# The two parts of the dense products' operand move into one tile at another place of the on-chip memory

## The chip, the cores and the metric

The kernel runs on one core of one Trainium2 chip. The metric is device time in microseconds (us) for one execution: 1100.3 us is the median of three executions before the change.

## What is computed

The reference is two transformer blocks on one sequence of 256 tokens with 1024 features, in float32. Cut to what matters here, every layer is a chain of dense products with attention, scans and convolutions between them:

```python
h = rmsnorm(x, gain)
y = h @ w_in                       # queries, keys, values, gates: thousands of columns
x = x + mix(y) @ w_out             # mix: attention, gated linear attention, convolution
h = rmsnorm(x, gain)
x = x + square(relu(h @ w_up)) @ w_down      # 1024 -> 4096 -> 1024
```

There are three such layers with three MLPs, and a norm at the end.

## The kernel before

Features lie on the 128 partitions, tokens along them: an operand of 1024 features is eight K tiles of 128 features by 256 tokens. The weights come from the chip's main memory as one stream of 128 by 128 blocks, in the order of use, through three 1 MB staging buffers (`stg`, issued from SyncE's queue).

A product in float32 is made of three products in the matrix unit's float32r format. Each weight block is split into a high part `whi` (ScalarE, L168) and a low part `wlo` (VectorE, L170); the operand is split likewise into `xh` and `xl`, by `operand(j, gain)` for K tile j (ScalarE L299, VectorE L300). `gemm` then issues per K tile, back to back: `whi` with `xh` (L225), `whi` with `xl` (L228), `wlo` with `xh` (L229). In each the weight block is loaded (128 columns, a row of its own in the trace, engine PEld), and the operand's K tile of 256 columns streams past it (engine PE).

- `gemm1` and `gemm2` make one or two output tiles by eight K tiles in this way. They serve all projections (`xh`, `xl`), the mixing products (`yc_h`, `ya_h`, `yh_h`, `mh`, `oh`, `cq_h`, `ck_h` and their low parts) and the MLP's first product.
- `gemm_tokens` (L264) turns the roles round: a 128 token piece of `xh` or `xl` is loaded as the weights, and 256 columns of `whi` or `wlo` stream past it.
- `gemm_wide` (L237, L238) serves the MLP's second product, except for the last of its eight output tiles: the hidden values lie in one tile `hid`, with high and low part next to each other for each K tile, so that one matmul takes 512 columns of both.
- The last output tile of the MLP's second product goes through `gemm1` with `hid[:, :, 0]` and `hid[:, :, 1]`.

Side work (attention, scans) is cut in steps that are put in between the tiles of the dense products; its small matmuls run on TensorE between those of the products.

Where things lie. Buffers are laid out one behind the other along each partition in the order in which the program asks for them, each on a multiple of 32 bytes. In the program of before, `xv` (constants and the residual stream, 8504 bytes per partition) comes first at byte 16512, `xh` (8192 bytes) follows at 25024, `xl` at 33216, `cst` at 41408. The five `whi` buffers begin at 76800 and the five `wlo` buffers at 97280, 4096 bytes each; a block of 128 columns is 512 bytes, so every weight block begins on a multiple of 512. The other operands begin at: `oh` 128000, `ol` 136192; `hid` 128000 in the first two MLPs and 136192 in the third; `ya_h`, `ya_l`, `yh_h`, `yh_l`, `yc_h`, `yc_l` from 128000 to 148480 in steps of 4096; `cq_h` 188928, `cq_l` 192000; `ck_h` 201216, `ck_l` 203264; `mh` 204576, `ml` 212768. K tiles of these are 1024 bytes apart (`hid`: 2048).

Of the kernel before, what the change touches and what calls it, by code (L numbers as in the profile page):

```python
# [35 lines left out]
# output tiles of the MLP's second product, from the last, that take one part of the operand at a time  # L36
WN = 1
# columns of the first weights to come
FIRST = 256
# steps of side work per tile of eight blocks, in three places  # L40
# [24 lines left out]
def _mid(ap, n):  # L65
    """[p, f] -> [p, n, f], the same f for each of n."""
    return ap.unsqueeze(1).to_broadcast([ap.shape[0], n, ap.shape[1]])


def _last(ap, n):  # L70
    """[..., f] -> [..., f, n], each of f repeated n times."""
    return ap.unsqueeze(len(ap.shape)).to_broadcast(list(ap.shape) + [n])
# [3 lines left out]
def kernel(  # L76
# [36 lines left out]
    xh = keep.tile([128, KD, T], FP32R, name="xh")  # L113
    xl = keep.tile([128, KD, T], FP32R, name="xl")
# [9 lines left out]
    # the first products want the first K tiles of both operands  # L124
# [29 lines left out]
    def first(chain, ready=4, n=2):  # L154
        """Keep the splits of the weights that come after the next `ready` units behind a chain of small steps."""
        hold[:] = [None] * ready + [chain] * n

    def take(u, pieces=2):
        """The parts of unit u."""
        c, i = divmod(u, CHUNK_UNITS)  # L160
        if c not in staged:
            load(c)
        src = staged[c][:, i * UW:(i + 1) * UW]
        h = whi_p.tile([128, UW], FP32R, name="whi")
        l = wlo_p.tile([128, UW], FP32R, name="wlo")
        n = UW // pieces
        pieces = [slice(q * n, (q + 1) * n) for q in range(pieces)]
        act = [nc.scalar.activation(out=h[:, z], in_=src[:, z], func=AF.Copy)  # L168
               for z in (pieces if u == 0 else [slice(0, UW)])]
        dve = [nc.vector.tensor_tensor(out=l[:, z], in0=src[:, z], in1=h[:, z], op=ALU.subtract) for z in pieces]  # L170
        chain = hold.pop(0) if hold else None
        if chain:
            after(act[0], chain[0])
            after(dve[0], chain[1])
        units.clear()
        units[u] = h, l

    def block(n=1):
        """The parts of the next n blocks, which lie in one unit."""
        b = stream["block"]  # L180
        stream["block"] = b + n
        u, i = divmod(b, UNIT)
        assert i + n <= UNIT
        if u not in units:
            take(u)
        h, l = units[u]
        return h[:, i * 128:(i + n) * 128], l[:, i * 128:(i + n) * 128]
# [33 lines left out]
    def gemm(ps, ks, ah, al, prev=None):  # L221
        """ps = W.T @ a over the K tiles ks; three of the four products of the parts."""
        for k in ks:
            h, l = block()
            m0 = nc.tensor.matmul(out=ps, lhsT=h, rhs=ah[:, k], start=(k == ks[0]), stop=False)  # L225
            if k == ks[0]:
                after(m0, prev)
            nc.tensor.matmul(out=ps, lhsT=h, rhs=al[:, k], start=False, stop=False)  # L228
            m1 = nc.tensor.matmul(out=ps, lhsT=l, rhs=ah[:, k], start=False, stop=(k == ks[-1]))  # L229
        return m1  # L230

    def gemm_wide(kt, a):
        """[128, 2, T] of which the halves' sum is W.T @ a, both parts of a[:, k] at once."""
# [22 lines left out]
    def gemm_tokens(kt, ah, al, dst, scale=None, steps=1):  # L256
        """dst(b) [128, 256] = (a.T @ W)[128 * b:] for 256 columns of W, times scale[:, b]: tokens on partitions."""
# [16 lines left out]
    def rsqrt(src, n, inv_n, dst, room=None):  # L274
        """dst = (src * inv_n + EPS) ** -0.5 over [128, n]: exp(-ln/2) and a Newton step."""
# [8 lines left out]
    def softplus_neg_abs(dst, z):  # L284
        """dst = ln(1 + exp(-|z|))"""
# [4 lines left out]
    def sigmoid(dst, z, t):  # L290
        """dst = exp(min(z, 0) - ln(1 + exp(-|z|)))"""
# [5 lines left out]
    def operand(j, gain):  # L297
        """Operand parts of x[:, j] * gain."""
# [6 lines left out]
    def squares(j):  # L305
        """The squares of x[:, j] on top of those before."""
# [22 lines left out]
    def rstd_tokens():  # L329
        """rtok[t, b] = rstd of token 128 * b + t"""  # L330
# [8 lines left out]
    def residual(ah, al, groups, gain):  # L339
        """x += W.T @ a, and the next norm's operand. All tiles take the first group of K tiles, then  # L340
        all the second: the operand's last K tiles may come late."""
# [9 lines left out]
    def mlp(gain_next):  # L351
# [6 lines left out]
        with ExitStack() as st:  # L358
# [11 lines left out]
            for j in range(KD):  # L370
                # the sum of the parts costs a step, which the last tile does without
# [5 lines left out]
                # the last tile of all goes on in halves of the tokens  # L377
# [18 lines left out]
    def v_natural(dst, vT, rows):  # L396
        """dst[:, kt, :] = vT[:, kt * 128:].T"""
# [8 lines left out]
    def scores(qT, kT, rows, parts=None):  # L406
        """[128 queries, 384]: block 0 with keys 0..127, block 1 with keys 0..255."""
# [13 lines left out]
    def softmax(ps, add0, add1):  # L421
        """exp of scores + additive terms, less their greatest, over the sums."""
# [21 lines left out]
    def pv(po, pT, v, cols):  # L444
        """po [64, 256] = (P @ v).T: keys 0..127 for all queries, keys 128..255 for queries 128..255."""
# [3 lines left out]
    class Pair:  # L449
        """Two heads whose outputs fill one K tile of the next product: probs(g) gives [128, 384] of weights,  # L450
        v the values, oh and ol the parts to fill."""
# [23 lines left out]
    def pipeline(pairs, d):  # L475
        """The heads of the pairs one step apart: logits and softmax, d steps later transposes, then values."""
# [14 lines left out]
    # ================= block 1 =================  # L491
# [16 lines left out]
    with ExitStack() as st:  # L508
# [13 lines left out]
        # -- sparse attention: index queries and keys, then keys, values and queries --  # L522
# [27 lines left out]
        def select():  # L550
            """Index scores (block 0 in columns 0..127, block 1 in 128..383) and what they leave out."""
# [15 lines left out]
            # the 64 greatest of each row, the lower index first among equals, become TAKEN  # L567
# [11 lines left out]
        def unit_heads(j0, n):  # L579
            """Norms of keys (tile 0) and queries (1..4) per head, in place."""  # L580
# [31 lines left out]
        def sparse():  # L612
# [8 lines left out]
            # heads j (keys of group 0) and j + 4 (group 1) lie in one tile  # L621
# [27 lines left out]
        # -- gated linear attention --  # L649
# [10 lines left out]
        # the lower bound is zero for every input: a softmax over the one layer, less itself  # L660
# [23 lines left out]
        def factors(b):  # L684
            """Decays to and from the token b - 1 of each 2 * b, each at most one, on keys and queries."""
# [12 lines left out]
        def decays():  # L698
            # products of queries and keys with their decay, a level of block sizes at a time
# [6 lines left out]
            for li, b in enumerate(sizes):  # L706
# [7 lines left out]
                elif b in (64, 32):  # L714
                    # keys of each first half by queries of each second half
# [44 lines left out]
        # -- short convolution --  # L760
# [19 lines left out]
        # -- gates and the branches' products --  # L780
# [40 lines left out]
    # rotary angles less whole turns: position * frequency, in rows of 16 frequencies (the first half negated)  # L821
# [25 lines left out]
    # ================= block 2, layer 0 =================  # L847
    first(rsqrt(sum_squares(), T, 1.0 / D, rstd))
    with ExitStack() as st:
# [6 lines left out]
        # a query sees all keys of its own chunk of 64 and of those before  # L856
        nc.gpsimd.tensor_tensor(out=cb[:, :, 128:256], in0=cb[:, :, 128:256], in1=_mid(chunkm[:, 128:256], 8), op=ALU.add)

        # forget gates: running sums of log sigmoid, one row per head
# [11 lines left out]
        # the sums of the queries, tokens on partitions  # L871
# [11 lines left out]
        # both parts of the sums, and ones that pick a head's row of each  # L883
# [55 lines left out]
    # ================= block 2, layer 1 =================  # L939
    first(rsqrt(sum_squares(), T, 1.0 / D, rstd))  # L940
    with ExitStack() as st:
# [6 lines left out]
        def rope(z, parts):  # L948
            """z * cos + (halves of each 32 rows exchanged) * sin, in place; returns the two terms' tiles."""
# [6 lines left out]
        # latent queries and keys  # L956
# [43 lines left out]
        def stick(j, slot_):  # L1000
            def probs(g):
# [7 lines left out]
                # softplus(z) summed from the key before the query down to each key  # L1009
# [33 lines left out]
        # queries: two tiles of four heads' rotary parts, four tiles of two heads' plain parts  # L1043
# [14 lines left out]
        # keys' plain parts and values in pairs  # L1058
# [38 lines left out]
def _blocks(w, tiles, rows=None):  # L1097
    """Weight columns in tiles of 128 (an int is the first of 128; a list of runs is zero-padded), each as [128, K / 128, 128]."""
# [13 lines left out]
def _stream(i):  # L1112
    """All weights, block after block in the kernel's order of use."""
# [11 lines left out]
    def add_tokens(w, tiles):  # L1125
        """Two tiles, a block of each in turn."""
# [15 lines left out]
    # attention heads lie in pairs (j, j + 4)  # L1142
# [36 lines left out]
    # pairs of heads in the order in which the kernel ends them (0..3 stick-breaking, 4..7 latent)  # L1179
# [44 lines left out]
def _constants():  # L1224
# [9 lines left out]
    # running sums start again at the key before the query, and at the end of block 0's keys  # L1234
# [14 lines left out]
def _toeplitz(rows, index):  # L1249
    """[heads, n] -> [128, heads, 256]: queries 128..255 by keys 0..255, at index(query - key)."""  # L1250
# [38 lines left out]
```

## Time and profile before

| | |
|---|---|
| three executions | 1099.16, 1100.3, 1103.56 us |
| median | 1100.3 us |
| profiled execution: first to last instruction (its span) | 1098.2 us |
| median less span: what lies around the span, and the spread of executions | 2.1 us |
| TensorE matmul (PE) busy | 1078.4 us, 98% of the span |
| weight loads (PEld) busy | 1008.0 us, 92% |
| VectorE (DVE), ScalarE (ACT), GpSimd (POOL) busy | 833.4, 600.9, 151.2 us |
| mean granted clock of TensorE | 0.998 of 2.4 GHz |

The profiled execution has no time of its own beside its span. A matmul's row has the moment at which it begins and a modelled duration, and matmuls overlap: the duration of one (276 to 283 ns for 256 columns) is longer than the step from the beginning of one to that of the next. The step is the pace; it is read from the moments in the time line, or from a stretch: the stretch's length plus one duration, over the number of matmuls that a row counts in it.

### The profile page before, as it was taken

Reading aid. Unit: us, or ns where it says so; the run is one execution under the profiler, and the core shown is the slowest. Engines: PE = TensorE matmul, PEld = TensorE weight load, DVE = VectorE, ACT = ScalarE, POOL = GpSimd, SP = SyncE. Lnnn points to the kernel's source line nnn. Section 1 sums busy time; section 2 is a strip of 40 time slices with the busy share of each in tenths; the row PEclk is TensorE's granted clock in tenths of the full one; section 3 lists DMA queues with packets and bytes.
Section 4 is the critical chain, followed back from the end, with each engine's and each line's share of the span. In section 5 each row is a group of like instructions: output and inputs, shape, how many; then the busy total and the mean of one; then the engine's idle time right before and its main releaser. Section 6 shows DMA issues by size and latency. Waiting matters only on the chain. (4 is left out here: it accounts for less than half of the span.)

```text
span 1098.2 us, 20294 instructions
## 1 busy us (share of the span) xinstructions
PE 1078.4 (98%) x8132; PEld 1008.0 (92%) x8132; DVE 833.4 (76%) x1606; ACT 600.9 (55%) x943; POOL 151.2 (14%) x164
## 2 busy tenths in 40 slices
PE   7999999999999999999999999999999999999996
PEld 6998989999999988998888999988999889999886
DVE  7999798887986666687667866666689679776663
ACT  6467456665565544455554555444458655555441
POOL 1035450110300001110001200011021004000110
PEclk9999999999999999999999999999999999999999
DMA  8543333454455554563333545455454323555541
GB/s 308 201 164 135 127 144 132 181 192 155 169 216 192 192 179 179 184 226 116 116 116 116 191 179 181 182 189 192 154 192 154 116 93 142 209 195 195 186 174 39
DMA packets 29007, 183.94 MB, mean 167 GB/s; under 512 B 3056, under 2 KB 6384, under 8 KB 7280
## 3 DMA queue, kind: packets, MB, share of 16 engines
q1 hardware_dynamic: 28768, 182.50, 45.7%
q8 instruction: 64, 1.05, 0.4%
q14 instruction: 31, 0.25, 0.1%
q10 hardware_dynamic: 144, 0.13, 0.0%
HBM read 181.57 MB, written 1.05 MB: 166 GB/s over the span
## 5 line engine op out<-in xcount | busy, mean ns | idle before, releaser
L170 DVE TENSOR_TENSOR wlo<-stg,whi 128x512 fp32r<-128x512 f32 (+1 forms) x676 | 473.3, 741 | 164.9 <-ACT whi L168 160.8
L168 ACT ACTIVATE whi<-stg 128x1024 fp32r<-128x1024 f32 (+1 forms) x340 | 356.2, 1051 | 343.7 <-PE pg L228 195.7
L225 PE MATMUL pg<-xh,whi 128*128 128x256 f32 x1472 | 416.0, 283 | 7.2 <-ACT whi L168 6.8
L229 PE MATMUL pg<-xh,wlo 128*128 128x256 f32 x1472 | 414.1, 282 | 0.6 <-DVE wlo L170 0.6
L228 PE MATMUL pg<-xl,whi 128*128 128x256 f32 x1472 | 413.3, 281 | 0.6 <-DVE xl L300 0.6
L225 PEld LDWEIGHTS pg<-xh,whi 128*128 128x128 f32 x1472 | 277.4, 189 | 12.6 <-ACT whi L168 7.1
L229 PEld LDWEIGHTS pg<-xh,wlo 128*128 128x128 f32 x1472 | 279.4, 190 | 2.7 <-DVE wlo L170 1.3
L228 PEld LDWEIGHTS pg<-xl,whi 128*128 128x128 f32 x1472 | 277.9, 189 | 3.3 <-issue 1.2
L237 PE MATMUL pg<-hid,whi 128*128 128x512 f32 x672 | 236.1, 396 | 0.0
L238 PE MATMUL pg<-hid,wlo 128*128 128x256 f32 x672 | 188.5, 281 | 0.0
L237 PEld LDWEIGHTS pg<-hid,whi 128*128 128x128 f32 x672 | 126.1, 188 | 30.1
L238 PEld LDWEIGHTS pg<-hid,wlo 128*128 128x128 f32 x672 | 127.0, 189 | 0.0
L308 POOL TENSOR_TENSOR sqa<-xv 128x256 f32<-128x256 f32 x6 | 4.3, 720 | 480.3 <-DVE xv L384 300.1
L312 POOL TENSOR_TENSOR sq<-xv 128x256 f32<-128x256 f32 x36 | 27.7, 776 | 175.6 <-DVE xv L384 171.7
L429 ACT ACTIVATE p<-p,m 128x128 f32<-128x128 f32 x64 | 28.5, 446 | 23.1 <-DVE m L427 22.8
L228 PE MATMUL pg<-ol,whi 128*128 128x256 f32 x128 | 37.1, 292 | 0.0
L264 PE MATMUL pg<-whi,xh 128*128 128x256 f32 x128 | 37.1, 290 | 0.0
L313 POOL TENSOR_TENSOR sqa<-sqa,sq 128x256 f32<-128x256 f32 x36 | 36.7, 1019 | 2.4
L225 PE MATMUL pg<-oh,whi 128*128 128x256 f32 x128 | 36.0, 291 | 0.5 <-ACT oh L271 0.5
L229 PE MATMUL pg<-oh,wlo 128*128 128x256 f32 x128 | 36.2, 285 | 0.0
L369 DVE TENSOR_TENSOR hid<-s,hid 128x512 fp32r<-128x512 f32 x48 | 33.1, 690 | 4.0
L264 PE MATMUL pg<-wlo,xh 128*128 128x256 f32 x128 | 35.9, 281 | 0.0
(344 smaller groups left out, 1565.1 us busy)
## 6 DMA issues: line engine op xcount, KB each, us to landing
stg<-w SPq DMA_DIRECT2D x168, 1024.0 KB, 4.8
t<-t_bias SPq DMA_DIRECT2D x8, 128.0 KB, 2.8
cb<-chk_bias SPq DMA_DIRECT2D x1, 1024.0 KB, 4.7
xv<-x_in SPq DMA_DIRECT2D x2, 384.0 KB, 6.1
cst<-consts SPq DMA_DIRECT2D x1, 640.0 KB, 10.9
stg<-w SPq DMA_DIRECT2D x1, 512.0 KB, 7.8
out<-xg SPq DMA_DIRECT2D x2, 256.0 KB, 2.5
stg<-w SPq DMA_DIRECT2D x1, 384.0 KB, 6.5
```

The lines of the kernel that those rows point to most:

```text
L168: act = [nc.scalar.activation(out=h[:, z], in_=src[:, z], func=AF.Copy) for z in (pieces if u == 0 else [slice(0, UW)])]
L170: dve = [nc.vector.tensor_tensor(out=l[:, z], in0=src[:, z], in1=h[:, z], op=ALU.subtract) for z in pieces]
L225: m0 = nc.tensor.matmul(out=ps, lhsT=h, rhs=ah[:, k], start=(k == ks[0]), stop=False)
L228: nc.tensor.matmul(out=ps, lhsT=h, rhs=al[:, k], start=False, stop=False)
L229: m1 = nc.tensor.matmul(out=ps, lhsT=l, rhs=ah[:, k], start=False, stop=(k == ks[-1]))
L237: nc.tensor.matmul(out=ps, lhsT=h, rhs=a[:, k], start=(k == 0), stop=False)
L238: nc.tensor.matmul(out=ps[:, 1], lhsT=l, rhs=a[:, k, 0], start=False, stop=(k == kt - 1))
L264: nc.tensor.matmul(out=ps, lhsT=a[:, k, t], rhs=w_, start=(k == 0 and i == 0), stop=(k == kt - 1 and i == 2))
L312: nc.gpsimd.tensor_tensor(out=s, in0=x[:, j], in1=x[:, j], op=ALU.mult)
L313: nc.gpsimd.tensor_tensor(out=sqa, in0=sqa, in1=s, op=ALU.add)
L369: nc.vector.tensor_tensor(out=hid[:, j:j + 2, 1], in0=s, in1=hid[:, j:j + 2, 0], op=ALU.subtract)
L429: nc.scalar.activation(out=p[:, a:b], in_=p[:, a:b], func=AF.Exp, scale=-1.0, bias=m[:, i:i + 1], accum_out=sums[:, i:i + 1])
```

## The change

`xh` and `xl` are no longer tiles of their own. One tile `xo` holds both, K tile by K tile: high part of K tile 0, low part of K tile 0, high part of K tile 1, and so on. It is asked for ahead of `xv`, so it lies where `xv` lay.

```diff
-    xv = keep.tile([128, NVEC + KD * T], FP32, name="xv")
+    xo = keep.tile([128, KD, 2, T], FP32R, name="xo")
+    xh, xl = xo[:, :, 0], xo[:, :, 1]
+    xv = keep.tile([128, NVEC + KD * T], FP32, name="xv")
     vec = xv[:, 0:NVEC]
     x = xv[:, NVEC:].rearrange("p (k t) -> p k t", k=KD)
-    xh = keep.tile([128, KD, T], FP32R, name="xh")
-    xl = keep.tile([128, KD, T], FP32R, name="xl")
     cst = keep.tile([128, NCONST], FP32, name="cst")
```

All other lines of the diff take out comments and docstrings. The code behind moves down by one line (L225 becomes L226).

## Rows read from the trace of the kernel before

**Rows 1.** The page's first part: busy time, share of the span, instructions.

```profile
span 1098.2 us, 20294 instructions
PE 1078.4 (98%) x8132; PEld 1008.0 (92%) x8132; DVE 833.4 (76%) x1606; ACT 600.9 (55%) x943; POOL 151.2 (14%) x164
```

**Rows 2.** Waits of TensorE: us in total, times, longest.

```profile
PE pg L225 <- ACT whi L168: 6.8, 2, 5.0
```

**Rows 3.** Groups by shape on PE, whole span: count | busy us, mean ns.

```profile
L225 PE MATMUL pg<-xh,whi 128*128 128x256 f32 x1472 | 416.0, 283 | 7.2 <-ACT whi L168 6.8 <-DVE xv L347 0.4
L264 PE MATMUL pg<-whi,xh 128*128 128x256 f32 x128 | 37.1, 290 | 0.0
```

**Rows 4.** Stretches, PE: us, busy (count), PEclk, DMA share, GB/s; MLPs' first product.

```profile
300.00:360.00 60.00, 60.00 (x512) 1.00 0.56 198
620.00:680.00 60.00, 60.00 (x512) 1.00 0.55 195
930.00:990.00 60.00, 60.00 (x532) 1.00 0.57 210
```

**Rows 5.** The same in the three MLPs' second product (`gemm_wide`).

```profile
386.00:446.00 60.00, 60.00 (x341) 1.00 0.52 191
706.00:766.00 60.00, 60.00 (x341) 1.00 0.51 184
1006.00:1066.00 60.00, 60.00 (x348) 1.00 0.52 187
```

**Rows 6.** Time line of PE in the third MLP: start us, us.

```profile
953.77 0.28 PE L229 MATMUL pg<-xh,wlo 128*128 128x256 f32 x1
...
954.90 0.28 PE L225 MATMUL pg<-xh,whi 128*128 128x256 f32 x1
```

**Rows 7.** Time line of PE in the first MLP.

```profile
339.74 0.28 PE L229 MATMUL pg<-xh,wlo 128*128 128x256 f32 x1
...
340.92 0.28 PE L225 MATMUL pg<-xh,whi 128*128 128x256 f32 x1
```

**Rows 8.** Time line of PE: attention output product of block 2.

```profile
594.79 0.28 PE L228 MATMUL pg<-ol,whi 128*128 128x256 f32 x1
...
595.99 0.28 PE L229 MATMUL pg<-oh,wlo 128*128 128x256 f32 x1
```

**Rows 9.** Stretches, PE: end of the last MLP; tokens product; mixing product with `mh`.

```profile
1078.00:1086.00 8.00, 8.00 (x69) 1.00 0.01 2
66.00:76.00 10.00, 10.00 (x88) 1.00 0.41 148
264.00:284.00 20.00, 20.00 (x173) 1.00 0.38 133
```

**Rows 10.** Time line of PE around two small matmuls of the side work.

```profile
197.78 0.28 PE L225 MATMUL pg<-xh,whi 128*128 128x256 f32 x1
...
198.91 0.28 PE L228 MATMUL pg<-xl,whi 128*128 128x256 f32 x1
199.03 0.59 PE L751 MATMUL sc<-mm,ones 128*128 128x256 f32 x2
199.27 0.47 PE L229 MATMUL pg<-xh,wlo 128*128 128x256 f32 x1
199.58 0.28 PE L225 MATMUL pg<-xh,whi 128*128 128x256 f32 x1
...
200.52 0.28 PE L229 MATMUL pg<-xh,wlo 128*128 128x256 f32 x1
```

**Rows 11.** Weight loads by shape, three stretches (300, 930, 594 us): count | busy, mean ns.

```profile
L229 PEld LDWEIGHTS pg<-xh,wlo 128*128 128x128 f32 x170 | 32.6, 192 | 0.0
...
L229 PEld LDWEIGHTS pg<-xh,wlo 128*128 128x128 f32 x177 | 33.2, 188 | 0.0
...
L229 PEld LDWEIGHTS pg<-oh,wlo 128*128 128x128 f32 x17 | 3.3, 192 | 0.0
```

**Rows 12.** Time line of PE: first and last matmul of the `xh`, `xl` products.

```profile
5.00 0.58 PE L225 MATMUL pg<-xh,whi 128*128 128x256 f32 x1 [5.00 <-ACT whi L168]
...
998.99 0.28 PE L229 MATMUL pg<-xh,wlo 128*128 128x256 f32 x1
```

## The prediction

> **What bounds the kernel now.** I read the page's first part first. TensorE's matmuls fill 98% of the span, its weight loads 92%; every other engine has at least a quarter of the span free [rows 1]. The list of waits comes next, to see whether that share is real: the longest wait on TensorE is 6.8 us, nearly all of it at the start, before the first operand is there [rows 2]. So the time is TensorE's, and what makes a matmul step longer or shorter makes the kernel longer or shorter by the same amount. The groups by shape show where the steps are: three lines with 1472 matmuls each take `xh` or `xl` as the moving operand, 4416 in all, and 3 × 128 = 384 more load a piece of them as weights [rows 3]. The busy time in these rows is modelled and overlaps, so I do not use it as a price. I use the pace.
>
> Then I compared the pace of one and the same product in three places. In the third MLP's first product 532 matmuls fall into 60 us, in the first and second 512 [rows 4]: (60 + 0.276) / 532 = 113.3 ns a step against (60 + 0.281) / 512 = 117.7 ns. The granted clock is 1.00 in all three, DMA's share nearly the same. The time line confirms it: ten steps take 1.13 us in one place [rows 6] and 1.18 us in the other [rows 7]. The same code on the same buffers has two paces, each held for a whole MLP. Other operands have a third: ten steps with `oh` and `ol` take 1.20 us, 120.0 ns [rows 8], and so do the `hid` products at the end, (8 + 0.283) / 69 [rows 9]. No operand is missing in these stretches and nothing waits; it is the same instruction at the same clock.
>
> What differs is the address. The weights always begin on a multiple of 512 bytes. `xh` and `xl` lie 448 bytes past such a multiple; `oh`, `ol` and `hid` lie exactly on one, and so do five more pairs (`ya`, `yh`, `yc`, `cq`, `ck`). All seven pairs settle at 120. `mh` and `ml` lie 288 past one and step at (20 + 0.28) / 173 = 117 [rows 9]. The weight loads go along: 188 ns where the pace is fast, 192 for one of three loads where it is slow, 192 with `oh` [rows 11]. My reading, a theory so far: the load of the next weights and the moving operand's stream run at the same time, and hold each other up when they reach the same part of the memory at once; where the two begin relative to each other sets how often.
>
> **The change part by part.** *Instructions.* None is removed, added or moved, no DMA changes size or queue; each write and read of `xh[:, k]` and `xl[:, k]` touches the same contiguous 1 KB as before, so there is no new wait. Cost: nothing, and no cover is needed. ScalarE, VectorE and the first DMA meet `xv` and `xo` at other places; a few ns on some hundred instructions of engines that have slack [rows 1]; I take nothing, at most ±1 us at the start, where TensorE waits [rows 2].
>
> *The address of the operand.* `xo` takes `xv`'s place at 16512, and K tiles and parts are steps of 1024 from there: all begin 128 bytes past a multiple of 512. Behind `xo` and `xv` nothing moves, since the two together are as long as before. No row of before has an operand at 128, so the price is bounded from both sides by the paces that rows show: 120.0 [rows 8, 9] and 113.3 [rows 4].
>
> I need the present mix for it. Between the first and the last of the 4416 matmuls [rows 12] I read the steps from their start times: 2051 are fast (mean 113.4), 2197 slow (mean 117.9), and 168 are over 126 ns, with a wait or a side matmul inside; those I leave alone. The 384 with exchanged roles step at about 117 to 118 [rows 9].
>
> - All at 120: 2051 × 6.6 + 2197 × 2.1 + 384 × 2.2 ns = 13.5 + 4.6 + 0.8 = 19 us longer.
> - All at 117.8: 2051 × 4.4 ns = 9 us longer.
> - All at 113.3: 2197 × 4.6 ns = 10 us shorter, and 384 × 4.4 ns = 1.7 us more if the exchanged roles follow.
>
> I take the upper bound, 120. The new place is a multiple of 128 bytes, as are all seven pairs that step at 120, while the only operands that step faster (`xh` and `xl` at 64 past such a multiple, `mh` and `ml` at 32) are not. That is the nearest row; but those seven are multiples of 512 too, so the rows cannot tell a rule of 128 from one of 512.
>
> *The `gemm_wide` products.* Their operand does not move, but their pace goes with that of the product before: 341 matmuls in 60 us in the first two MLPs, 348 in the third [rows 5], that is 2 × 60.3 / 341 = 354 against 347 ns per K tile. Of 672 K tiles 448 are slow. What state they will start in is unknown: from 448 × 6.7 = 3 us shorter to 224 × 6.7 = 1.5 us longer. I take nothing.
>
> *A rule that speaks against all this.* The rows show one instruction form at 113, 118 and 120 ns [rows 4, 8]. The Trainium skill, "SBUF — State Buffer", section "Who interferes with whom", says that TensorE has two independent read ports, one for the moving operand and one for weight loads, and never waits on anyone; by that the address is free and the sum is 0 instead of 19 us. The trace does not agree that every step costs the same, though it does not show the cause.
>
> The sum is 1100.3 + 19.0 = 1119.3 us. It is made on the profiled execution, whose span of 1098.2 us stands 2.1 us under the median; the added steps lie inside the span, so I put them on the median.
>
> **The rivals.**
>
> *Faster: the streams no longer meet.* A matmul reads 1024 bytes while the load reads 512, so an operand that begins 64 bytes behind (448) catches the load early, and one that begins 128 bytes ahead runs away from it. If places repeat only every 256 or 512 bytes, they meet late or hardly at all, and the fast pace holds everywhere. This decides from the point where the repeat is longer than 128 bytes and a late meeting costs no more than an early one. For it: the fast pace exists and lasted a whole MLP [rows 4]. Against it: exchanged roles put the moving operand 64 bytes ahead, and that product steps at 117, never fast for long [rows 9]. Time: 10 + 1.7 + 3 us shorter at most, 1086; 1090 without the last two.
>
> *A little slower: late meetings cost as in `mh` and in the exchanged roles.* Everything settles near 117.8: 9 to 10.5 us longer, 1109 to 1111. For it: two different distances, 288 and 64 ahead, both give that pace [rows 9]. Against it: 120 has more operands.
>
> *Nothing changes.* The two paces alternate at the new place as at the old. A switch is seen where small matmuls come between: eleven products at 113 ns, two side matmuls, then 117.5 [rows 10]. One MLP that switches costs 768 × 4.4 + 224 × 6.7 ns = 4.9 us, about the spread of the three executions shown, so 1095 to 1105, and 1100 is the middle. By the skill's rule above the time would also be 1100.
>
> **How the numbers follow.** 120 everywhere 0.34; 117.8 everywhere 0.18; fast everywhere 0.30; two paces as before, or no effect of the address, 0.18 (0.12 and 0.06). The predicted time is that of the first, 1119; its own range is 1114 (exchanged roles stay, `gemm_wide` all fast) to 1122 (`gemm_wide` all slow, and the spread of executions). The range over all cases is 1087 to 1121: it cuts the fastest part of the fast case and the top of the first, about 0.15 together. 0.5%, 5.5 us, is about what a measurement can tell from no change. Slower by more: 0.34 + 0.18 and 0.03 of the fourth, 0.55; within: 0.13; faster: 0.30 and 0.02, 0.32.
>
> **What would show it.** Right: in the three stretches of the MLPs' first product about (60 + 0.283) / 0.120 = 502 matmuls in 60 us, in each, and weight loads of 192 ns on all three lines; `oh`, `hid` and `mh` as before. 512 in each would show the second case, 532 the fast one, a mixture the fourth. The counts of instructions, the waits and the other engines' busy times stay. I am wrong from the start if those change, that is if another order of instructions came out; and wrong in the main step if an operand 128 bytes past a multiple of 512 does not behave like one on it.

## The result and the profile after

After the change the median is 1110.72 us (1109.84 to 1111.3 in four executions) against 1100.19 us (1099.16 to 1103.56, four executions of before): a ratio of 1.0097 with a 95% interval from 1.0078 to 1.0115. The kernel is 10.5 us slower.

The page's first part of the kernel after, to be read against [rows 1]:

```profile
span 1108.7 us, 20294 instructions
PE 1089.3 (98%) x8132; PEld 1020.1 (92%) x8132; DVE 834.5 (75%) x1606; ACT 601.6 (54%) x943; POOL 151.2 (14%) x164
```

The counts of instructions are the same on every engine, VectorE, ScalarE and GpSimd are busy as long as before to within 1.1 us, and TensorE has 10.9 us more in a span that is 10.5 us longer. TensorE's matmuls come in the same order with the same shapes, so the addresses are what differs. The first of the waits on TensorE, to be read against [rows 2]:

```profile
PE pg L226 <- ACT whi L169: 7.1, 2, 4.9
```

So the time did not go into waiting. Stretches of PE in the three MLPs' first products, which answer to [rows 4] (length, busy time and count, granted clock, DMA share, GB/s):

```profile
300.00:360.00 60.00, 60.00 (x508) 1.00 0.54 189
620.00:680.00 60.00, 60.00 (x508) 1.00 0.55 197
930.00:990.00 60.00, 60.00 (x508) 1.00 0.55 193
```

(60 + 0.28) / 508 = 118.7 ns a step, in all three. It is a pace that no row of before showed: slower than both of [rows 4], faster than the 120.0 of [rows 8]. The time line in the first MLP, to be read against [rows 7]:

```profile
339.73 0.28 PE L226 MATMUL pg<-xo,whi 128*128 128x256 f32 x1
...
341.27 0.28 PE L229 MATMUL pg<-xo,whi 128*128 128x256 f32 x1
```

There are 13 steps between these two, 1.54 / 13 = 118.5 ns. Weight loads of the first MLP, to be read against [rows 11]:

```profile
L230 PEld LDWEIGHTS pg<-xo,wlo 128*128 128x128 f32 x169 | 31.8, 188 | 0.0
L229 PEld LDWEIGHTS pg<-xo,whi 128*128 128x128 f32 x169 | 31.8, 188 | 0.0
L226 PEld LDWEIGHTS pg<-xo,whi 128*128 128x128 f32 x169 | 31.8, 188 | 0.0
```

None of them has the 192 ns that the loads with `oh` had at 120.0 ns. And the `gemm_wide` stretches, to be read against [rows 5]:

```profile
386.00:446.00 60.00, 60.00 (x348) 1.00 0.52 192
710.00:770.00 60.00, 60.00 (x341) 1.00 0.52 179
1014.00:1074.00 60.00, 60.00 (x348) 1.00 0.52 191
```

One MLP more than before runs at the faster of its two paces.

The account closes. Read from their start times (each matmul counted from its own start to that of the next), the 4416 products with `xh` or `xl` took 548.4 us instead of 536.8 (11.6 more), the 384 with exchanged roles 48.2 instead of 47.7 (0.5 more), the `gemm_wide` products 1.5 us less. Each other product and all small matmuls took the same to 0.1 us. 11.6 + 0.5 - 1.5 = 10.6, against 1108.7 - 1098.2 = 10.5 us of span.

### The profile page after: what moved, and what is told of

Read it like the earlier page. It is cut to its first block, busy times and chain, and to the rows that moved or that the text cites. A ratio compares the mean times of both kernels' runs of the same rounds, so it can differ in the third digit from the quotient of the medians.

```text
span 1108.7 us, 20294 instructions
## 1 busy us (share of the span) xinstructions
PE 1089.3 (98%) x8132; PEld 1020.1 (92%) x8132; DVE 834.5 (75%) x1606; ACT 601.6 (54%) x943; POOL 151.2 (14%) x164
## 4 chain that ended last, share of the span: by engine, by line
PE 92%; DVE 5%; issue 1%; DMA 1%; POOL 1%; ACT 0%; SPq 0%; DVEq 0%
PE pg L226 19%; PE pg L229 19%; PE pg L230 19%; PE pg L238 14%; PE pg L239 7%; PE pg L265 5%; PE po L447 2%; DVE wlo L171 2%; PE sc L417 2%; PE sc L410 1%; PE pt L440 1%; PE sc L732 1%; PE po L448 1%; DMA stg<-w 1%; DVE xo L301 1%
## 5 line engine op out<-in xcount | busy, mean ns | idle before, releaser
L226 PE MATMUL pg<-xo,whi 128*128 128x256 f32 x1472 | 419.6, 286 | 7.5 <-ACT whi L169 7.1
L230 PE MATMUL pg<-xo,wlo 128*128 128x256 f32 x1472 | 417.8, 284 | 0.6 <-DVE wlo L171 0.4
L229 PE MATMUL pg<-xo,whi 128*128 128x256 f32 x1472 | 416.9, 284 | 0.5 <-DVE xo L301 0.5
L226 PEld LDWEIGHTS pg<-xo,whi 128*128 128x128 f32 x1472 | 277.5, 189 | 12.9 <-ACT whi L169 7.4
L229 PEld LDWEIGHTS pg<-xo,whi 128*128 128x128 f32 x1472 | 277.8, 189 | 3.1 <-issue 1.2
L230 PEld LDWEIGHTS pg<-xo,wlo 128*128 128x128 f32 x1472 | 277.6, 189 | 2.7 <-DVE wlo L171 1.3
L265 PE MATMUL pg<-whi,xo 128*128 128x256 f32 x256 | 48.3, 288 | 0.0
L265 PEld LDWEIGHTS pg<-whi,xo 128*128 128x128 f32 x256 | 39.5, 189 | 1.5 <-issue 0.5
L226 PE MATMUL pg<-oh,whi 128*128 128x256 f32 x128 | 36.0, 291 | 0.5 <-ACT oh L272 0.5
L265 PE MATMUL pg<-wlo,xo 128*128 128x256 f32 x128 | 36.3, 283 | 0.0
```

The lines of the kernel that those rows point to most:

```text
L265: nc.tensor.matmul(out=ps, lhsT=a[:, k, t], rhs=w_, start=(k == 0 and i == 0), stop=(k == kt - 1 and i == 2))
```

## The experiments

All kernels here compute the full result.

**Layout or address?** The change does two things at once: it puts the parts side by side, and it moves them from 448 to 128 bytes past a multiple of 512. Each was done alone. In the first kernel the one tile stands behind `xv`:

```diff
-    xo = keep.tile([128, KD, 2, T], FP32R, name="xo")
-    xh, xl = xo[:, :, 0], xo[:, :, 1]
     xv = keep.tile([128, NVEC + KD * T], FP32, name="xv")
     vec = xv[:, 0:NVEC]
     x = xv[:, NVEC:].rearrange("p (k t) -> p k t", k=KD)
+    xo = keep.tile([128, KD, 2, T], FP32R, name="xo")
+    xh, xl = xo[:, :, 0], xo[:, :, 1]
```

> One tile for both parts as after the change, but behind xv, so that it begins 448 bytes past a multiple of 512 as xh and xl did before. Theory A (the address alone sets the pace): the two paces of before come back, 113 and 118 ns a step, 532 or 512 matmuls in 60 us of an MLP's first product, and the time is within 5 us of before, 1095 to 1105 us. Rival B (the order of the parts in memory does it: high and low part 1024 bytes apart instead of 8192): 508 matmuls in 60 us as after the change, 1110 us.

In the second, two tiles stand ahead of `xv`:

```diff
-    xo = keep.tile([128, KD, 2, T], FP32R, name="xo")
-    xh, xl = xo[:, :, 0], xo[:, :, 1]
+    xh = keep.tile([128, KD, T], FP32R, name="xh")
+    xl = keep.tile([128, KD, T], FP32R, name="xl")
     xv = keep.tile([128, NVEC + KD * T], FP32, name="xv")
```

> Two tiles as before the change, but ahead of xv, so that both begin 128 bytes past a multiple of 512. Theory A (the address alone): 508 matmuls in 60 us in all three MLPs' first products and 1110 us, as after the change. Rival B (the order in memory): 512 or 532 in 60 us, 1100 us.

One tile at the old place: 1104.28 us, ratio to before 1.0004 (0.9977 to 1.0031). Two tiles at the new place: 1111.19 us, ratio 1.0082 (1.0054 to 1.011). Before took 1104.07 us beside them (1094.55 to 1105.38). Stretches of PE of the first kernel, then of the second; the first shows the slow one of before's paces in all three, and the fast one elsewhere, 113.5 to 113.7 ns from 220 to 260 us:

```profile
300.00:360.00 60.00, 60.00 (x511) 1.00 0.56 203
620.00:680.00 60.00, 60.00 (x512) 1.00 0.56 199
930.00:990.00 60.00, 60.00 (x512) 1.00 0.56 199
```

```profile
300.00:360.00 60.00, 60.00 (x508) 1.00 0.53 187
620.00:680.00 60.00, 60.00 (x506) 1.00 0.54 193
930.00:990.00 60.00, 60.00 (x508) 1.00 0.55 193
```

The 506 holds one step of 308 ns; without it the pace is 118.7 ns as in the other two stretches. The address alone does it; rival B falls. Whether the two parts lie 1024 or 8192 bytes apart has no effect on the pace.

**Which addresses?** Five kernels give each layer's operand a place of its own inside a tile with 512 bytes to spare, so that one execution shows three places in the three MLPs (below with the places of the first; `layer` counts the projections and the MLP of a layer one after the other):

```diff
-    xo = keep.tile([128, KD, 2, T], FP32R, name="xo")
-    xh, xl = xo[:, :, 0], xo[:, :, 1]
+    # bytes past a multiple of 512 at which the operand of each of the six layers begins
+    PAST = [0, 0, 32, 32, 64, 64]
+    xr = keep.tile([128, KD * 2 * T + 128], FP32R, name="xo")
+    layer = [-1]
+
+    class Part:
+        def __init__(self, p):
+            self.p = p
+
+        def __getitem__(self, i):
+            o = (PAST[layer[0]] - 128) % 512 // 4
+            return xr[:, o:o + KD * 2 * T].rearrange("p (k h t) -> p k h t", k=KD, h=2)[:, :, self.p][i]
+
+    xh, xl = Part(0), Part(1)
...
     def operand(j, gain):
+        if j == 0:
+            layer[0] += 1
```

> The operand begins at another distance past a multiple of 512 bytes in each layer: 0 in block 1's projections and the first MLP, 32 in the second layer and second MLP, 64 in the third. Theory A with places that repeat every 512 bytes: at 0 the pace of the other operands there, 120 ns, 502 matmuls in 60 us of the first MLP; at 32 and 64 between 113 and 119, 505 to 532. If only multiples of 128 were slow: 502 in the first MLP, 512 to 532 in the other two. Rival B (the order in memory): 508 in all three.

> The same with distances of 96, 160 and 192 bytes for the three pairs of layers. Theory A with a repeat of 512: three different counts in 60 us of the MLPs' first products, somewhere from 505 to 532. With a repeat of 128: 96 as in a pure distance of 32 bytes behind, 160 like the 32 of the run before and 192 like its 64. Rival B: 508 in all three.

> Operand at 224 (block 1, first MLP), 256 (second layer, second MLP) and 288 bytes (third) past a multiple of 512. If places repeat every 256 bytes: at 256 the 120.0 ns of distance 0, 502 matmuls in 60 us of the second MLP's first product, and at 288 the 116.7 ns of distance 32, 516 in the third; 224 is new. If they repeat every 512: other paces than those at 0 and 32.

> Operand at 320, 352 and 384 bytes past a multiple of 512. Repeat of 256: the paces of 64, 96 and 128, that is 117.8, 120.0 and 118.7 ns, or 512, 502 and 508 matmuls in 60 us of the three MLPs' first products. Repeat of 512: at least one of them differs, for instance a faster third MLP.

> Operand at 416, 448 and 480 bytes past a multiple of 512. Repeat of 256: 118.7 ns at 416 as at 160 (508 matmuls in 60 us), 113.3 or 117.8 at 448 as before and at 192 (532 or 512), and at 480 what 224 gave. Repeat of 512: 416 or 480 with a pace of its own.

The five took 1109.52, 1107.14, 1112.07, 1111.85 and 1110.1 us, one execution each. Stretches of PE in their MLPs' first products, one fence for each kernel in this order, so at 0, 32, 64; 96, 160, 192; 224, 256, 288; 320, 352, 384; 416, 448, 480 bytes:

```profile
303.00:363.00 60.00, 60.00 (x502) 1.00 0.55 193
623.00:683.00 60.00, 60.00 (x517) 1.00 0.56 202
931.00:991.00 60.00, 60.00 (x512) 1.00 0.58 196
```

```profile
303.00:363.00 60.00, 60.00 (x502) 1.00 0.54 193
623.00:683.00 60.00, 60.00 (x508) 1.00 0.56 195
931.00:991.00 60.00, 60.00 (x532) 1.00 0.59 208
```

```profile
303.00:363.00 60.00, 60.00 (x510) 1.00 0.55 193
623.00:683.00 60.00, 60.00 (x503) 1.00 0.55 199
931.00:991.00 60.00, 60.00 (x516) 1.00 0.55 194
```

```profile
303.00:363.00 60.00, 60.00 (x512) 1.00 0.56 197
623.00:683.00 60.00, 60.00 (x502) 1.00 0.56 199
931.00:991.00 60.00, 60.00 (x508) 1.00 0.54 193
```

```profile
303.00:363.00 60.00, 60.00 (x508) 1.00 0.55 193
623.00:683.00 60.00, 60.00 (x512) 1.00 0.53 193
931.00:991.00 60.00, 60.00 (x510) 1.00 0.57 203
```

Read the counts in pairs 256 bytes apart: 0 and 256 give 502 and 503, 32 and 288 give 517 and 516, 64 and 320 give 512 twice, 96 and 352 give 502 twice, 128 and 384 give 508 each (128 in the kernel after), 160 and 416 give 508, 224 and 480 give 510. At 192 the third MLP has 532, at 448 the second has 512: the two paces of before. So the pace depends on the place modulo 256. A repeat of 128 is excluded, because 0 gives 502 and 128 gives 508. The weight loads' durations, which the prediction had named as a sign, do not tell the pace: at 96 bytes they are 187 to 190 ns, at 0 bytes 192 ns, and both places step at 120 ns.

**How fine?** Two more of these kernels, at 176, 208 and 200, and at 184, 216 and 16 bytes:

> Operand at 176 (block 1, first MLP), 208 (second layer, second MLP) and 200 bytes (third) past a multiple of 512, all close to the one distance, 192, that has shown the fast pace. Theory: meetings are counted in pieces of 16 bytes or more, so that 200 acts as 192 (113.3 or 117.8 ns, 532 or 512 matmuls in 60 us of the third MLP's first product), while 176 and 208 have paces of their own between 113 and 120. Rival: the pace changes with every few bytes, and 200 has one of its own as well.

> Operand at 184, 216 and 16 bytes past a multiple of 512. Theory of pieces of 16 bytes: 184 acts as 176 of the run beside it and 216 as its 208; 16 has a pace between 116.7 (32) and 120 (0). Rival: 184 and 216 have paces that neither 176 nor 208 shows; if one of these gives 113.3 ns in the whole of its layers, it is the better place.

They took 1110.7 and 1115.0 us, one execution each. Their stretches, one fence each:

```profile
303.00:363.00 60.00, 60.00 (x505) 1.00 0.54 193
623.00:683.00 60.00, 60.00 (x506) 1.00 0.56 197
931.00:991.00 60.00, 60.00 (x503) 1.00 0.56 195
```

```profile
303.00:363.00 60.00, 60.00 (x502) 1.00 0.54 193
623.00:683.00 60.00, 60.00 (x500) 1.00 0.54 193
931.00:991.00 60.00, 60.00 (x508) 1.00 0.56 193
```

The theory of 16 byte pieces falls as I had put it: 200 has 503, not the 512 or 532 of 192; 184 has 502 where 176 has 505; 216 has 500 where 208 has 506. The places that are not a multiple of 16 are among the slowest here. None of the six is faster than 192 in these stretches. Outside these stretches there is an exception: in the last kernel's third layer, at 16 bytes, 69 of 99 steps from 800 to 820 us took 113 or 114 ns, before the MLP's first product settled at 118.7. So 192 is not the only distance at which the fast pace occurs.

**Operand or distance?** So far the weights stood still. Now they move to 320 bytes past a multiple of 512, and the norms' operand to 256, by four small fillers (each set to zero once):

```diff
+    gap = pool("gap").tile([128, 16], FP32, name="gap")
+    nc.vector.memset(gap, 0.0)
     whi_p = pool("whi", 5)
     wlo_p = pool("wlo", 5)
+    rest = pool("rest").tile([128, 48], FP32, name="rest")
+    nc.vector.memset(rest, 0.0)
...
+    front = keep.tile([128, 32], FP32, name="front")
+    nc.vector.memset(front, 0.0)
     xo = keep.tile([128, KD, 2, T], FP32R, name="xo")
...
+    back = keep.tile([128, 32], FP32, name="back")
+    nc.vector.memset(back, 0.0)
```

> The weights' high and low parts move to 320 bytes past a multiple of 512, the operand of the norms to 256; so all moving operands, also oh, hid and the other pairs that did not move, begin 192 (or 448, which is 192 modulo 256) bytes ahead of the weights, counted modulo 512; mh is an exception. Theory A1 (the distance between operand and weights sets the pace): oh, ol and the hid products leave 120 ns for 113 to 118, the norms' operand too, and the time is 1075 to 1095 us. Rival A2 (the place of the operand by itself sets the pace): oh and hid stay at 120.0 ns, the norms' operand goes to the 120 ns of its new place, a multiple of 256, and the time is near 1119 us.

The time is 1097.46 us (1093.7 to 1101.18) against 1100.22 us of before beside it, ratio 0.996 (0.994 to 0.998): a little faster, but slower than the 1075 to 1095 us that theory A1 had given. `oh` still begins on a multiple of 512 here; the weights moved against it. Its time line, to be read against [rows 8]:

```profile
569.78 0.28 PE L238 MATMUL pg<-oh,wlo 128*128 128x256 f32 x1
...
572.16 0.28 PE L238 MATMUL pg<-oh,wlo 128*128 128x256 f32 x1
```

There are 21 steps between, 2.38 / 21 = 113.3 ns instead of 120.0. This pace does not last: behind some matmuls of the side work the same product steps at 2.59 / 22 = 117.7 ns.

```profile
583.36 0.28 PE L238 MATMUL pg<-oh,wlo 128*128 128x256 f32 x1
...
585.95 0.28 PE L234 MATMUL pg<-oh,whi 128*128 128x256 f32 x1
```

Over both blocks the steps of `oh` and `ol` up to 126 ns have a mean of 115.5 ns instead of 119.5. The weights' new place is not simply better for every operand: `mh`, whose distance went from 32 to 224 (modulo 256), went from 117.8 to 118.3 ns. The norms' operand, at a multiple of 256, has no trace of the 503 that scan_c shows there; stretches in the three MLPs' first products, and in `gemm_wide`:

```profile
303.00:363.00 60.00, 60.00 (x532) 1.00 0.59 207
623.00:683.00 60.00, 60.00 (x532) 1.00 0.58 208
931.00:991.00 60.00, 60.00 (x512) 1.00 0.54 192
...
386.00:446.00 60.00, 60.00 (x341) 1.00 0.53 189
706.00:766.00 60.00, 60.00 (x342) 1.00 0.50 179
1006.00:1066.00 60.00, 60.00 (x342) 1.00 0.52 191
```

So it is the distance between operand and weights that counts, and A2 falls. The gain is small for two reasons. The norms' operand keeps its two paces, and here two MLPs have the fast one instead of one, but block 1's projections from 200 to 260 us have the slow one (512 matmuls in these 60 us); all in all the 4416 products took 536.4 us against 536.8. And `gemm_wide` ran at its slower pace in all three MLPs, 1.5 us more than in before's profile. What was gained is mainly `oh` and the other operands that left 120 ns: 48.3 us against 49.6 for `oh` and `ol`, 0.6 for the products of the last `hid` tile, which now step at 117.8 ns, 0.2 each for `yc`, `ya`, `yh`, `cq`.

**The two paces at one distance.** The kernel of before once more:

> The kernel of before once more, for its profile alone: executions of it between 1094.6 and 1105.4 us were seen beside the other runs. Theory (two paces at distance 448, either of which a stretch may settle in): every one of the three MLPs' first products has 512 or 532 matmuls in 60 us and gemm_wide 341 or 348, nothing in between, in another selection than 512, 512, 532; each MLP that changes moves the span by 4.9 us against 1098.2. Rival (the spread comes from somewhere else, waits or the clock): 512, 512, 532 again with another span.

Its span is 1102.8 us, and its stretches in the MLPs' first products are:

```profile
300.00:360.00 60.00, 60.00 (x512) 1.00 0.57 198
620.00:680.00 60.00, 60.00 (x512) 1.00 0.55 195
930.00:990.00 60.00, 60.00 (x512) 1.00 0.56 197
```

The third MLP has changed from 532 to 512, and its `gemm_wide` from 348 to 342 in 60 us. The span is 4.6 us longer: 2.8 us in the products with `xh` or `xl`, 1.5 us in `gemm_wide`. The prediction had put one such switch at 4.9 us. The same program settles now in one pace, now in the other.

The executions of before show the same without a trace. The 29 that ran beside il_448 and all_192 fall in three groups with nothing between: two at 1094.55 and 1094.87 us, nine from 1099.26 to 1100.27, eighteen from 1103.36 to 1105.38. The groups are some 4.8 us apart, about one switch of an MLP; that this is what separates them was seen in the profiles of the two upper groups only. The size of the result hangs on it: three of the four executions of before beside the result are of the middle group. Against before_again's span the kernel after is 1108.7 - 1102.8 = 5.9 us longer, not 10.5.

## Why the prediction came out as it did

*What bounds the kernel.* Right: a change of addresses alone made TensorE's busy time and the span longer by 10.9 and 10.5 us, with no new wait.

*That the address changes the pace, and the order of the parts does not.* Right, by il_448 and sep_128. The Trainium skill ("SBUF — State Buffer", "Who interferes with whom") gives TensorE two independent read ports and has it wait on no one. What the prediction drew from it, that the address is free, does not hold here: in all_192 `oh`, with the weights moved against it, stepped at 113.3 and 117.7 ns instead of 120.0. The measurement decides; whether a port waited, no run shows.

*"I take the upper bound, 120."* This is the step that was off, in size; by the prediction's own sign (an operand 128 bytes past a multiple of 512 behaves like one on it, 502 matmuls in each stretch) the main step is wrong, since the stretches have 508. It rested on the new place being a multiple of 128 bytes, like the seven pairs at 120. Those are multiples of 256 (of 512 even), and places repeat every 256 bytes: 128 past such a multiple gives 118.7 ns. With the measured pace the prediction's own sum is 2051 × 5.3 + 2197 × 0.8 + 384 × 1.3 ns = 10.9 + 1.8 + 0.5 = 13.2 us instead of 19; start times show 12.1 for these products, since some steps with a side matmul inside got shorter. The prediction had said that its rows could not tell a rule of 128 from one of 512; both were wrong, and scan_a to scan_e show 256. The sum also took before's third MLP at its fast pace as given, but that pace is a matter of the execution.

*The range.* The time of 1110.72 us lies below the main case's own range, 1114 to 1122. It lies inside the range over all cases, 1087 to 1121, because that range was made wide enough for the rivals. The direction was forecast with its reason, the address; that the number falls inside is owed to that width.

*`gemm_wide`, taken as nothing.* One MLP changed to its faster pace, 1.5 us less, inside the bounds given. 13.2 - 1.1 - 1.5 = 10.6.

*The rivals.* "A little slower" gave 1109 to 1111 us and the time is 1110.72, but at 118.7 ns with 1.5 us back from `gemm_wide`, not at 117.8. "The streams no longer meet" did not happen: an operand 128 bytes ahead is slower than one 64 bytes behind. Its condition, a repeat longer than 128 bytes, is met; its second one, that a late meeting costs no more, is not, if meetings are the cause at all. "Nothing changes" fails at the new place, where all three MLPs have one and the same pace; its price for a switch at the old place, 4.9 us, was met by 4.6. This fits the spread of before, 1094.55 to 1105.38 us beside il_448, and the smaller one of the kernel with two tiles at 128, 1110.46 to 1113.79: there the pace of the `xh`, `xl` products is one, and sep_128's profile differs from that of the kernel after by 3.4 us, of which 3.0 are `gemm_wide` in its slower pace.

*What is open.* That two streams hold each other up is argued, not shown: shown is that the pace changes with the distance between moving operand and weights, modulo 256 bytes. The distance alone does not fix it. 192 has two paces, 16 showed 113 to 114 as well as 118.7, and `mh`, at 32 like `xo` in scan_a, steps at 117.8 instead of 116.6. Why, and what picks one of two, was not settled; the switches in [rows 10] come after small matmuls of the side work, but no run forced one.

## What to carry to other kernels

Where TensorE fills the span with weight load and matmul in turn, count the matmuls in equal stretches: different counts at the same clock, without a wait, are a reason to look where operand and weights lie (and to profile a second execution, since here one and the same program showed two counts). Of the 14 distances tried the best made 113.3 ns a step in some stretches, 117.7 in others, and the worst over 120, up to 6% more. Moving the weights so that every operand but `mh` stood at the best, with fillers of 512 bytes in all, gave 0.4% of the kernel's time. And before a move of buffers is judged, look where everything lies afterwards: the layout was blameless, the place decided.

## What the runs showed of the hardware

The pace of a 128 by 128 weight load with 256 columns of float32r, by the bytes that the operand begins ahead of the weights (its address less theirs), modulo 256, each from one count above by (60 + 0.28) over the count. All are stretches of an MLP's first product; a count is good to about one matmul, 0.2 ns, and 16 is the third MLP of scan_g:

| ahead | 0 | 16 | 32 | 64 | 96 | 128 | 160 | 176 | 184 | 192 | 200 | 208 | 216 | 224 |
|---|---|---|---|---|---|---|---|---|---|---|---|---|---|---|
| matmuls in 60 us | 502 | 508 | 517 | 512 | 502 | 508 | 508 | 505 | 502 | 532 or 512 | 503 | 506 | 500 | 510 |
| ns a step | 120.1 | 118.7 | 116.6 | 117.7 | 120.1 | 118.7 | 118.7 | 119.4 | 120.1 | 113.3 or 117.7 | 119.8 | 119.1 | 120.6 | 118.2 |

I had not expected an order without a simple slope (96 bytes as slow as 0), nor that one distance has two steady paces, either of which can last through the first product of an MLP, some 80 us.
